# Opening of a hybrid flow step: modulation computed from column blocks on three engines, x of four tiles turned by layout with norms as broadcast rows, loads in a fixed order

## The chip, the cores and the metric

The kernel runs on one core of a Trainium2 chip. A core has a matrix engine (TensorE, PE in the profile), a vector engine (VectorE, DVE), a scalar engine (ScalarE, ACT), a general engine (GpSimd, POOL) and a queue engine (SyncE, SP) that issues most DMAs. Each engine executes its own list of instructions in order and waits on semaphores for the others. The metric is the device time of one execution in microseconds (us). The kernel before took 2190.32 us, the median of three runs (2189.26 to 2190.99).

## The reference

One step of a backbone with two groups of tokens: 128 context tokens (`x_prompt`, conditioned by `c_ctx`) and 2048 latent tokens (`x_sample`, conditioned by `c`). D is 1024. The opening, which is what the change touches, computes for each group

```python
m = jnp.einsum('...d,de->...e', jax.nn.silu(cvec), w) + b      # w is w_ada (1024 x 3072), b is b_ada
shift, scale, gate = jnp.split(m, 3, axis=-1)
xn = rmsnorm(h, ln_g) * (1.0 + scale) + shift                  # h is x; the norm runs over D of each token
proj = jnp.einsum('btd,de->bte', xn, w_in)
```

The columns of `proj` go to three branches: a gated DeltaNet (its q, k, v, decays and the gate `z_a`), a spatial gating MLP, and a Fourier mixer. Each has a SiLU gate path; the branches are projected, merged by sigmoid gates, projected again, and added to x. Outputs are both groups' tokens after a last norm, and the DeltaNet states of the context.

## The kernel before, in words

**Tiles and number format.** The 2176 tokens are cut into five tiles (`TBS`): four of 512 latent tokens (called tiles 0 to 3 here) and one of the 128 context tokens (tile 4). The modulated x lives on chip for the whole kernel, transposed (D on partitions, in 8 blocks k; tokens along the row), as a sum of two 16-bit parts `xh` and `xl`. Weights are split likewise, scaled by a power of two that comes from their sum of squares (`converting`, lines 231 to 252: a ScalarE square with a sum, a small matmul and some one-column VectorE steps in `scales`, a ScalarE scaling that writes the high part, a VectorE pass that writes the low part). A product is three 16-bit matmuls (`gemm_T`, lines 263 to 269): high by high, high by low, low by high.

**The opening, lines 368 to 453.** `c` and `c_ctx` are loaded as 16 rows, transposed by PE, and made to `scT` (SiLU, with D on partitions). The first 2048 columns of `w_ada` come in 8 blocks of 256 columns, each in two loads of 512 KB (line 426) into 8 buffers. PE multiplies `scT` (2 columns, the stationary side) with each 256-wide row block; of blocks 0, 2, 4 and 6 the second half is summed by VectorE (`ada_sum`, lines 407 and 409) and then reduced by PE. The result (2 rows of 256) is copied (line 436) and transposed back in pairs into `pa` (line 438). Ahead of block 4 stand the load of x's first tile and five small loads of parameter columns (`columns`). Lines 443 to 453 then make `sh` and `ms`, the shift and the scale with the norm's gain, bound their size, and scale both by `sx`; `isx` is the reverse factor and goes into every weight's `w.inv` (line 249).

**The silu stage of branch A, lines 456 to 498.** `getw(4)` converts the four weight blocks of `z_a`, and `load_w` those of the decays; both are placed behind the last load of `w_ada` (`issue_after`, which orders instructions of one engine). For each tile: load x with tokens on partitions (line 416), four squares with sums (line 474), a root on GpSimd (line 204), four scalings on VectorE (line 478); for each k, four PE transposes (line 482) into a bank, a VectorE pass that applies `ms` and `sh` (line 484), a ScalarE cast to `xh` (line 485) and a GpSimd subtraction to `xl` (line 486); then for each of four output blocks g a `gemm_T`, a sigmoid (line 491), a product (line 492), and a store to DRAM (line 494).

**What follows.** Lines 631 to 660: 12 output blocks of q, k and v over the five tiles, with the decays worked in between (line 646 is the ScalarE pass that empties a bank). Then the DeltaNet chunks, the other two branches, the merges and the last projection.

**What sets the order.** The program is handed to a scheduler that simulates the engines, takes instructions by priority as their operands come ready, gives out buffers from each pool, and writes a fixed list for each engine. A block under `high_priority` goes ahead. A DMA is placed on the queue of the engine that issues it, and holds that queue while its buffer is taken.

Of the kernel before, what the change touches and what calls it, by code (L numbers as in the profile page):

```python
# [20 lines left out]
P = 128  # L21
# [17 lines left out]
VS = 2048.0  # L39
TBS = [(0, 512), (512, 512), (1024, 512), (1536, 512), (2048, 128)]  # L40
# [88 lines left out]
def _laid_out(inputs):  # L129
# [6 lines left out]
        "w_outb": _by_block(w_out, cols),  # L136
    }

# [6 lines left out]
def hybrid_flow_kernel(ctx: ExitStack, tc: tile.TileContext, x_prompt, x_sample, state_delta, c, c_ctx, ln_g, w_ada,  # L145
                       b_ada, w_blk, w_bd, conv_w, a_log, dt_bias, o_norm_g, sgu_norm_g, w_spatial, b_spatial, w_brb,
                       w_outb, final_g, consts, consts16, y_prompt, y_sample, new_state, dbg=None):
# [37 lines left out]
    SY.dma_start(cst, consts[:, 0:_CF])  # L185
# [39 lines left out]

    def read_w(src, nkt, cols=P, tag="w"):
        st = sb(wp, [P, nkt, cols], "wst" if cols == P else tag + "st", bufs=2 if cols == P else 1)
        SY.dma_start(st, src.rearrange("p (k c) -> p k c", c=cols))
        return st

    def converting(w, st, nkt, cols=P, hi=None, lo=None, tag="w", bufs=5):
# [17 lines left out]
        V.tensor_mul(w.inv, inv, isx)  # L249
        yield  # L250
        A.activation(w.hi, st, AF.Copy, scale=s)  # L251
# [119 lines left out]
    SY.dma_start(prc[0:8, :], c.rearrange("o (k p) -> (o k) p", p=P))  # L371
    SY.dma_start(prc[8:16, :], c_ctx.rearrange("(k p) -> k p", p=P))
    pp = bank(ps_x, [P, 2, KT])
    PE.transpose(pp.rearrange("p g k -> p (g k)"), prc, ident[:16, :16])
    sc = sb(cp, [P, 2, KT], "sc")
    A.activation(sc, pp, AF.Sigmoid)
    scT = sb(cp, [P, KT, 2], "scT")
    V.tensor_mul(scT.rearrange("p k g -> p g k"), sc, pp)
    NPRM = 65
    prm = sb(p0p, [NPRM, P], "prm", bufs=1)  # L380
    pc = sb(cp, [P, NPRM], "pc")

    def columns():
        SY.dma_start(prm[0:8, :], ln_g.rearrange("o (k p) -> (o k) p", p=P))
        SY.dma_start(prm[8:44, :], conv_w[0].rearrange("t (k p) -> (t k) p", p=P))
        SY.dma_start(prm[44:48, :], sgu_norm_g.rearrange("o (k p) -> (o k) p", p=P))
        SY.dma_start(prm[48:49, :], o_norm_g)
        SY.dma_start(prm[49:65, :], b_ada[0, 0:2 * D].rearrange("(k p) -> k p", p=P))
# [30 lines left out]
    for blk in range(8):  # L419
        if blk == XB:  # L420
            load_x(*TBS[0])
            columns()
# [1184 lines left out]
```

## Time and profile before

| | |
|---|---|
| three runs, median | 2190.32 us (2189.26 to 2190.99) |
| the profiled execution | 2187.72 us, span 2185.9 us |
| mean granted clock of PE | 0.991 |
| `w_ada` loads | 16 of 512 KB on SyncE, the first issued at 1.9 us |
| x loads | tile 0 issued at 9.6 us, tile 1 at 30.2, tile 2 at 53.4, tile 3 at 76.2, tile 4 at 105.5 |
| first matmul of the silu stage | 46.58 us |
| first matmul of q, k, v | 152.05 us |

How to read what is quoted further down. The page's part 1 gives the busy time of each engine, its share of the span, and its number of instructions; part 4 the shares of the chain that ended last. A row of stretches has its borders in us, its length, then busy time and number of instructions of PE, PE's weight loads (PEld), DVE, ACT and POOL, then the clock that PE was granted (1.00 is full), the mean busy share of the 16 DMA engines, and GB/s. A row of the timeline has the start, the length, engine, line, operation, what is written and read, shape and count, and in brackets how long the engine stood idle before it and what released it. A row of groups has line, engine, operation, written and read names, shape and count, then total busy time, mean ns of one, and the idle time before. A row of one line's instructions has shortest, median and longest in ns, then the first and last start. A row of waits has the total, the number and the longest in us. A row of DMA issues has the size of one and the us from issue to landing. Line 194 is the helper that issues every matmul.

### The profile page before, as it was taken

The numbers are of one execution on the slowest core, as the hardware profiler recorded it, in microseconds if no ns is written. First come the engines' busy times: TensorE is split into PE (matmuls) and PEld (weight loads), VectorE is DVE, ScalarE is ACT, GpSimd is POOL, SyncE is SP. The second block draws the span as 40 slices with busy tenths as digits, with TensorE's granted clock in tenths as the row PEclk, the third lists the DMA queues.
The fourth block names the chain that finished last, engine by engine and source line by source line (L and its number), as shares of the span: only waits on it lengthen the run. The fifth ranks groups of instructions, "written<-read, shape, count | busy, mean of one in ns | idle before, by whom it ended". The sixth has DMA issues, their size and how long they took to land.

```text
span 2185.9 us, 42789 instructions
## 1 busy us (share of the span) xinstructions
PE 2120.1 (97%) x16327; PEld 1214.5 (56%) x16327; DVE 1320.6 (60%) x3147; ACT 1025.1 (47%) x2365; POOL 721.0 (33%) x893
## 2 busy tenths in 40 slices
PE   7999999999999999999899999999999999999998
PEld 3564444455555577777555555555655444444444
DVE  5736844479878697466655555765674544233454
ACT  3535744365655673455534445655653422222332
POOL 1421332223334332443322223354542222112543
PEclk9999999999999999999899999999999999999999
DMA  8424822167776753444655556766764533334542
GB/s 284 152 87 158 280 100 101 61 212 232 259 214 221 216 166 101 122 131 133 217 158 165 163 157 190 236 188 220 210 198 154 169 122 130 118 102 123 173 149 106
DMA packets 233240, 365.11 MB, mean 167 GB/s; under 512 B 38369, under 2 KB 132938, under 8 KB 230986
## 3 DMA queue, kind: packets, MB, share of 16 engines
q1 hardware_dynamic: 180650, 267.38, 39.2%
q0 software_dynamic: 12688, 51.27, 6.5%
q10 hardware_dynamic: 39696, 43.72, 6.0%
q8 instruction: 128, 2.10, 0.4%
q14 instruction: 78, 0.64, 0.1%
HBM read 234.67 MB, written 127.62 MB: 166 GB/s over the span
## 4 chain that ended last, share of the span: by engine, by line
PE 50%; DVE 6%; DMA 5%; ACT 3%; issue 2%; POOL 1%; ACTq 0%; SPq 0%; POOLq 0%; DVEq 0%
PE b L194 49%; DMA st<-br 1%; DVE XB L814 1%; DVE E L815 1%; DMA wst<-in_w_brb_dram 1%; ACT nd L767 0%; DVE big L1385 0%; ACT big L1384 0%; DVE wlo L252 0%; DMA ei<-XB 0%; DMA wst<-mrg 0%; PE b L1078 0%; DMA wst<-in_w_blk_dram 0%; DMA sn<-n 0%; DMA XB<-nd 0%
## 5 line engine op out<-in xcount | busy, mean ns | idle before, releaser
L194 PE MATMUL b<-xh,whi 128*128 128x512 f16 (+1 forms) x1920 | 653.3, 349 | 6.5 <-DVE sg L1152 4.7
L194 PE MATMUL b<-xl,whi 128*128 128x512 f16 (+1 forms) x1920 | 653.6, 349 | 0.0
L194 PE MATMUL b<-xh,wlo 128*128 128x512 f16 (+1 forms) x1920 | 652.0, 348 | 0.0
L194 PEld LDWEIGHTS <-whi 128*128 128x128 f16 x3904 | 358.0, 98 | 337.7 <-issue 16.5
L194 PEld LDWEIGHTS <-wlo 128*128 128x128 f16 x1952 | 191.9, 98 | 178.5 <-issue 3.6
L194 PE MATMUL b<-big,bhi 128*128 128x512 f16 (+1 forms) x960 | 252.1, 348 | 3.3 <-ACT big L1384 3.1
L1424 POOL TENSOR_TENSOR mrow<-mrow,sg 128x512 f32<-128x512 f32 (+1 forms) x80 | 94.5, 1182 | 287.6 <-DVE sg L1423 171.2
L194 PE MATMUL b<-big,blo 128*128 128x512 f16 (+1 forms) x480 | 163.5, 348 | 0.0
L1414 ACT ACTIVATE sg<-b,winv 128x512 f32<-128x512 f32 (+1 forms) x120 | 74.2, 619 | 165.7 <-PE b L194 165.1
L194 PEld LDWEIGHTS <-xh 128*128 128x128 f16 x1496 | 117.1, 98 | 30.3 <-DVE yT L1337 1.6
L194 PEld LDWEIGHTS <-bhi 128*128 128x128 f16 x960 | 87.3, 98 | 78.6 <-issue 3.5
L655 POOL TENSOR_TENSOR cy<-cy,raw 128x545 f32<-128x545 f32 (+1 forms) x48 | 66.4, 1409 | 186.5 <-ACT raw L654 186.5
L1423 DVE SCALAR_TENSOR_TENSOR sg<-b,binv,sg 128x512 f32<-128x512 f32 (+1 forms) x80 | 53.4, 668 | 103.1 <-PE b L194 93.6
L208 DVE CAST wscb<-wss 128x1 bf16<-128x1 f32 x93 | 14.2, 153 | 157.9 <-ACT wlo L242 66.7
L194 PE MATMUL b<-whi,xh 128*128 128x128 f16 x544 | 92.8, 219 | 2.7 <-DVE yT L1337 1.5
L194 PE MATMUL b<-whi,xl 128*128 128x128 f16 x544 | 92.8, 219 | 0.0
L194 PE MATMUL b<-wlo,xh 128*128 128x128 f16 x544 | 92.8, 219 | 0.0
L194 PE MATMUL b<-wohi,ml 128*128 128x512 f16 (+2 forms) x248 | 91.7, 372 | 0.7 <-DVE ml L1495 0.7
L194 PE MATMUL b<-wohi,mh 128*128 128x512 f16 (+2 forms) x248 | 91.9, 372 | 0.0
L194 PE MATMUL b<-wolo,mh 128*128 128x512 f16 (+2 forms) x248 | 91.9, 372 | 0.0
L887 POOL COPY T<-ES 32x256 f16<-32x256 f16 x68 | 28.8, 423 | 190.3 <-DMA ES<-ei 156.6
L252 DVE SCALAR_TENSOR_TENSOR wlo<-wst,wsc,whi 128x1024 f16<-128x1024 f32 x52 | 72.7, 1401 | 27.9 <-ACT whi L251 27.1
(469 smaller groups left out, 4317.9 us busy)
## 6 DMA issues: line engine op xcount, KB each, us to landing
wst<-in_w_blk_dram SPq DMA_DIRECT2D x60, 512.0 KB, 5.2
qkv<-cy POOLq DMA_DIRECT2D x12, 1089.0 KB, 5.2
st<-br SPq DMA_DIRECT2D x48, 256.0 KB, 4.0
mrow<-mrg SPq DMA_DIRECT2D x18, 512.0 KB, 4.3
mrow<-mrg SPq DMA_DIRECT2D x16, 576.0 KB, 4.3
mrg<-mrow POOLq DMA_DIRECT2D x16, 576.0 KB, 3.7
dc<-dec SPq DMA_DIRECT2D x17, 512.0 KB, 7.0
kq<-qkv SPq DMA_DIRECT2D x34, 256.0 KB, 4.0
```

Of the source, the lines that this page charges most:

```text
L194: PE.matmul(out, l, r, start=start, stop=stop)
L208: V.tensor_copy(sb16, ss)
L252: V.scalar_tensor_tensor(w.lo, st, s, w.hi, ALU.mult, ALU.subtract)
L655: G.tensor_tensor(y[:, c0:c1], y[:, c0:c1], raw[:, 1 + c0:1 + c1], ALU.mult)
L814: V.tensor_tensor(t3, X3[:, 0:k, k:k + 1].to_broadcast([P, k, n_]), E3[:, k:k + 1, k:32].to_broadcast([P, k, n_]), ALU.mult)
L815: V.tensor_tensor(E3[:, 0:k, k:32], E3[:, 0:k, k:32], t3, ALU.subtract)
L887: G.tensor_copy(T16[rows(a0, b), :, :, b], ES[0:32, :, 2 * a0 + b, :, wT])
L1414: A.activation(sg, ps, AF.Sigmoid, scale=gw.inv)
L1423: V.scalar_tensor_tensor(sg, ps, binv[:, 1:2], sg, ALU.mult, ALU.mult)
L1424: G.tensor_tensor(mr, mr, sg, ALU.add)
```

## The change

The host lays out more. `w_ada`'s first 2048 columns come as 16 blocks of 128 columns (`w_adb`), seven of them with D on partitions (for PE), nine transposed, with the output columns on partitions. The parameter columns and both conditioning vectors come as one array of 81 columns (`cols`). x of tiles 1 to 4 comes turned, with D on partitions (`x_t`, `x_tp`); `x_sample` and `x_prompt` are still inputs.

The modulation is computed block by block in the order `ADA_ORDER`: seven blocks on PE (the block is the stationary side, 2 columns move), two on GpSimd (a product with a broadcast row of SiLU, summed by ScalarE), seven on VectorE (product and sum in one instruction). The broadcast rows `rowc` come from 16 small matmuls. x's first tile is loaded behind the third block, scaled by its norms and transposed by PE into `raw0` during the loads. The first two weight blocks of `z_a` are read ahead of the last four blocks and converted without `isx`, which is multiplied into `w.inv` later. Loads pass through `load`, which orders each behind the load before it.

In the silu stage, tile 0 is made from `raw0`. Tiles 1 to 4 are loaded twice, in rows for the norms and turned for the product; the norms become a row that is spread over the partitions (tile 1 by four matmuls, the others through DRAM), and no transposes are made. `silu_za` takes two output blocks at once for tile 0 and for the first pair of tile 1.

```diff
+ADA_PE = (0, 1, 2, 8, 9, 10, 11)
+ADA_G = (3, 12)
+ADA_ORDER = (0, 4, 8, 3, 5, 1, 6, 9, 12, 13, 2, 7, 14, 10, 15, 11)
...
-    SY.dma_start(cst, consts[:, 0:_CF])
+    first = SY.dma_start(cst[:, 0:P], consts[:, 0:P])
...
+    def load(dst, src):
+        if turn_of[0] is None:
+            return SY.dma_start(dst, src)
+        with tc.issue_after(turn_of[0].ins):
+            turn_of[0] = SY.dma_start(dst, src)
+        return turn_of[0]
...
-        V.tensor_mul(w.inv, inv, isx)
+        if isx is None:
+            w.own = inv
+        else:
+            V.tensor_mul(w.inv, inv, isx)
...
+    def norms(xs, shared=False):
+        xss = sb(p0p, [P, len(xs)], "xss")
+        for j, x in enumerate(xs):
+            jk = sb(p0p, [P, D], "xm", F16, bufs=4)
+            if shared and j % 2:
+                V.scalar_tensor_tensor(jk, x, 1.0, x, ALU.mult, ALU.mult, accum_out=xss[:, j:j + 1])
+            else:
+                A.activation(jk, x, AF.Square, accum_out=xss[:, j:j + 1])
+        rs = sb(p0p, [P, len(xs)], "rs")
+        rsqrt(rs, xss, 1.0 / D, len(xs))
+        return rs
...
+    def modulate(b, st):
+        if b in ADA_PE:
+            for k in range(KT):
+                mm(pa[:, ADA_PE.index(b), :], st[:, k * P:(k + 1) * P], scT[:, k, :], k == 0, k == KT - 1)
+            return
+        for g in range(2):
+            if b in ADA_G:
+                prod = sb(p0p, [P, D], "prod", bufs=1)
+                G.tensor_tensor(prod, st, rowc[g], ALU.mult)
+                A.activation(prod, prod, AF.Copy, accum_out=ada[:, b, g:g + 1])
+            else:
+                junk = sb(p0p, [P, D], "xm", F16, bufs=4)
+                V.scalar_tensor_tensor(junk, st, 1.0, rowc[g], ALU.mult, ALU.mult, accum_out=ada[:, b, g:g + 1])
+
+    for i, b in enumerate(ADA_ORDER):
+        if i == 3:
+            x0 = sb(p0p, [P, 4, D], "xt")
+            for j in range(4):
+                load(x0[:, j, :], xrows(j * P, P))
+        if i == 12:
+            read_next()
+            read_next()
+        st = sb(p0p, [P, D], "ab", bufs=8)
+        load(st, w_adb[b])
+        modulate(b, st)
+        if i == 5:
+            rs0 = norms([x0[:, j, :] for j in range(4)])
+            for j in range(4):
+                A.activation(x0[:, j, :], x0[:, j, :], AF.Copy, scale=rs0[:, j:j + 1])
+            for k in range(KT):
+                ps = bank(ps_mm, [P, 512])
+                for j in range(4):
+                    PE.transpose(ps[:, j * P:(j + 1) * P], x0[:, j, k * P:(k + 1) * P], ident)
+                A.copy(raw0[:, k, :], ps)
+    fetch(2)
+    while len(wdone) - len(wsteps) < 2:
+        weight_step()
+    read_next()
+    read_next()
+    x1 = row_blocks(*TBS[1])
...
+    load_xt(1)
+    behind = load(cst[:, P:_CF], consts[:, P:_CF])
+    bdst = read_w(w_bd, KT, 16, "d")
+    turn_of[0] = None
...
+    def row_scale(ti, xs):
+        t0, tn = TBS[ti]
+        rs = norms(xs, ti == 1)
+        if ti == 1:
+            ps = bank(ps_x, [P, 4, P])
+            for j in range(4):
+                mm(ps[:, j, :], rs[:, j:j + 1].to_broadcast([P, P]), ident)
+            rsb = sb(p0p, [P, tn], "rsb", bufs=1)
+            V.tensor_copy(rsb, ps.rearrange("p j t -> p (j t)"))
+            return rsb
+        G.dma_start(rsD[t0:t0 + tn].rearrange("(j p) -> p j", p=P), rs)
+        rsb = sb(p0p, [P, tn], "rsb", bufs=1)
+        SY.dma_start(rsb, rsD[None, t0:t0 + tn].to_broadcast([P, tn]))
+        return rsb
+
+    for ti, (t0, tn) in enumerate(TBS):
+        g = 0 if t0 < NS else 1
+        for k in range(KT):
+            hi, lo = xh[:, k, t0:t0 + tn], xl[:, k, t0:t0 + tn]
+            if ti:
+                x = xts[ti][:, k, :]
+                V.scalar_tensor_tensor(x, x, ms[:, k, g:g + 1], rsb, ALU.mult, ALU.mult)
+                act = A.activation(hi, x, AF.Identity, bias=sh[:, k, g:g + 1])
+                if k == 2:
+                    made = act
+                if k % 2:
+                    G.tensor_scalar(x, x, sh[:, k, g:g + 1], None, ALU.add)
+                    G.tensor_tensor(lo, x, hi, ALU.subtract)
+                else:
+                    with tc.high_priority() if ti == 1 else ExitStack():
+                        V.scalar_tensor_tensor(lo, x, sh[:, k, g:g + 1], hi, ALU.add, ALU.subtract)
+                continue
+            made = A.activation(hi, raw0[:, k, :], AF.Identity, scale=ms[:, k, g:g + 1], bias=sh[:, k, g:g + 1])
+            t = sb(p0p, [P, 512], "xm", bufs=4)
+            of = V.tensor_scalar(t, raw0[:, k, :], ms[:, k, g:g + 1], sh[:, k, g:g + 1], ALU.mult, ALU.add)
+            (V if k % 2 else G).tensor_tensor(lo, t, hi, ALU.subtract)
+        if ti == 0:
+            zaw.extend(wdone[:2])
...
+            silu_za(0, (0, 1), others)
...
+            with tc.issue_after(zaw[3].made.ins):
+                rsb = row_scale(1, x1)
+                bdw = convert(bdst, KT, 16, hi=bdp[:, :, 0:16], lo=bdp[:, :, 16:32], tag="d")
+            silu_za(0, (2, 3))
+        else:
+            if ti < 4:
+                xs = row_blocks(*TBS[ti + 1])
+                load_xt(ti + 1)
+            for gs in ((0, 1),) if ti == 1 else ((0,), (1,)):
+                silu_za(ti, gs)
+            if ti < 4:
+                with tc.issue_after(made.ins):
+                    rsb = row_scale(ti + 1, xs)
+            for g in range(2, 4):
+                silu_za(ti, (g,))
...
-    SY.dma_start(wsn, w_spatial[0].rearrange("g p q -> p g q"))
+    with tc.issue_after(behind.ins):
+        SY.dma_start(wsn, w_spatial[0].rearrange("g p q -> p g q"))
```

`others`, called inside the first `silu_za` at its sixth k, converts the third and fourth weight block of `z_a`, placed behind the last passes that make tile 0. `row_blocks` loads the rows of a tile as blocks of 128 tokens, `load_xt` the turned x of a tile.

171 lines of the change are left out of this document (81 added, 90 removed).

## The prediction

> **What bounds the kernel now.** I read the page first. The engine line says that PE is busy 97% of the span and that no other engine comes near; the chain that ended last is half PE matmul on line 194. So a stage is worth what it costs PE, in matmuls issued or in gaps.
>
> ```profile
> span 2185.9 us, 42789 instructions
> PE 2120.1 (97%) x16327; PEld 1214.5 (56%) x16327; DVE 1320.6 (60%) x3147; ACT 1025.1 (47%) x2365; POOL 721.0 (33%) x893
> PE 50%; DVE 6%; DMA 5%; ACT 3%; issue 2%; POOL 1%; ACTq 0%; SPq 0%; POOLq 0%; DVEq 0%
> ```
>
> Then I cut the opening into stretches (busy time per engine, granted clock, DMA share, GB/s).
>
> ```profile
> 0.00:10.00 10.00, 3.57 (x9) 1.19 (x10) 2.09 (x7) 1.47 (x2) 0.61 (x9) 1.00 0.81 258
> 10.00:20.00 10.00, 10.00 (x45) 3.86 (x44) 4.80 (x13) 0.00 (x0) 0.00 (x0) 1.00 1.07 375
> 20.00:35.00 15.00, 11.35 (x55) 4.31 (x53) 9.75 (x25) 4.60 (x8) 1.18 (x1) 1.00 1.08 350
> 35.00:40.00 5.00, 5.00 (x26) 2.04 (x24) 0.85 (x4) 2.30 (x4) 0.00 (x0) 1.00 1.02 406
> 46.00:48.00 2.00, 2.00 (x10) 1.56 (x11) 2.00 (x3) 2.00 (x5) 1.40 (x1) 0.55 0.00 0
> 0.00:153.00 153.00, 138.03 (x764) 71.17 (x765) 90.71 (x198) 70.69 (x127) 50.36 (x60) 0.99 0.52 181
> 153.00:435.00 282.00, 282.00 (x1776) 141.25 (x1775) 160.27 (x190) 140.26 (x203) 75.28 (x90) 1.00 0.40 139
> ```
>
> Up to 40 us the DMA engines are full: loads set the pace. From 153 us PE is full for 282 us, so work that reaches line 646 earlier keeps its lead there. In between lies the silu stage of branch A. Its corners are in the timeline:
>
> ```profile
> 34.76 1.89 PE L194 MATMUL b<-ast,scT 128*2 128x256 f32 x8 [1.41 <-DMA ast<-in_w_ada_dram]
> 41.59 0.17 DVE L443 TENSOR_TENSOR sh<-b,pc 128x16 f32<-128x16 f32 x1 [0.84 <-PE b L438]
> 43.91 0.23 DVE L453 TENSOR_SCALAR sh<-sh,xsc 128x16 f32<-128x16 f32 x1
> 46.58 0.59 PE L194 MATMUL b<-xh,zhi 128*128 128x512 f16 x1
> 152.05 0.38 PE L194 MATMUL b<-xh,whi 128*128 128x512 f16 x1
> ```
>
> The modulation is ready at 43.91 + 0.23 = 44.1 us, although PE's last wait for a piece of w_ada ended at 34.8: about 9 us go into matmuls, VectorE sums, copies and transposes behind the loads. The silu stage then runs to 152.05, which is 107.9 us. What PE must issue in it:
>
> ```profile
> L194 PE MATMUL b<-xl,zhi 128*128 128x512 f16 x128 | 48.2, 382 | 0.7 <-POOL xl L486 0.7
> L194 PE MATMUL b<-xl,zhi 128*128 128x128 f16 x32 | 5.3, 219 | 0.0
> 44.00:152.00 108.00, 18.27 (x124) 14.91 (x124) 0.98 0.35 122
> 90.22 0.38 PE L194 MATMUL b<-xh,zhi 128*128 128x512 f16 x1
> 91.30 0.38 PE L194 MATMUL b<-xh,zlo 128*128 128x512 f16 x1
> 96.92 1.25 PE L482 MATMUL b<-cst,xt 128*128 128x128 f32 x10
> ```
>
> Five steps lie between 90.22 and 91.30, 0.216 us each. Three products of 128 make 384 x 0.216 = 82.9 us; the 96 narrow ones are a quarter as wide, 5.3 us by width. The third row is line 482 alone: 124 transposes in the stage. Ten run in 1.25 us of which the last one's own 0.27 us is latency, so 0.109 us each and 13.5 us in all. Together 101.7 us; the other 6.2 us are gaps, mostly between 44 and 60 us, where tile 0 is made while PE waits and the clock stands at 0.55.
>
> **The change part by part.**
>
> *Modulation ready.* Ahead of the last column block now stand 0.12 MB of small loads, 16 blocks of 0.524 MB, x's first tile with 2.10 MB and two weight blocks with 1.05 MB: 11.65 MB. The first 10 us moved 2.58 MB; the remaining 9.07 MB take 22.3 us at 406 GB/s, 25.9 at 350, so the block lands between 32.3 and 35.9. I take 375 GB/s: 34.2. Behind it come eight f32 matmuls with a 128-column stationary side. The nearest row loads such weights:
>
> ```profile
> 174.32 0.85 PEld L194 LDWEIGHTS b<-tok,cst 128*128 128x128 f32 x6
> L1577 DVE SCALAR_TENSOR_TENSOR hh<-hh,hss,fg 128x1024 f32<-128x1024 f32 x16 | 21.5, 1349 | 13.4 <-POOL hss L204 13.3
> L1517 POOL TENSOR_TENSOR gt<-gb,inv 128x1024 f32<-128x1024 f32 x16 | 31.3, 1956 | 9.6 <-DMA gb<-gate 9.6
> L474 ACT ACTIVATE jk<-xt 128x1024 f16<-128x1024 f32 x17 | 17.9, 1051 | 19.3 <-DMA xt<-in_x_sample_dram 18.4 <-DMA xt<-in_x_prompt_dram 0.8
> L485 ACT CAST xh<-xm 128x512 f16<-128x512 f32 x32 | 19.2, 613 | 17.4 <-DVE xm L484 17.0
> ```
>
> 0.85 / 6 = 0.14 us each, 1.1 us for eight, and 7.9 us for all 56 among the loads. The VectorE block lands one block (1.4 us) before the last and takes two passes of 1.35 us, so it ends 1.3 us behind the last landing. From there the small chain that took 44.1 - 41.6 = 2.5 us stays: 34.2 + 1.3 + 2.5 = 38.0. The other VectorE passes (seven blocks, 14 x 1.35 = 18.9 us) replace sums of like size and stand under 30 us of loading; GpSimd's four products (4 x 1.96 = 7.8 us) too. ScalarE is the tight one, in order: four copies of broadcast rows, four squares, four scalings, eight copies of transposed x, four sums of products, two weight squares and two scalings, that is 16 of 1.05 and 12 of 0.61, 24 us and some read-outs between 6 and 38 us. Any late operand delays the rest. I put 1 us on it and take 39.0, a gain of 5.1. Bounds: all loads at the fast rate, 36.1 (gain 8.0); ScalarE behind until 44 (gain 0).
>
> The rate hangs on the layout: the slow stretch (350) held w_ada in pieces of 1 KB a row, the fast one (406) weights and x in 4 KB. [...]
>
> *Transposes leave PE.* The stage loses 124 x 0.109 = 13.5 us and gains four 128-column f32 matmuls that spread the norm of tile 1 (4 x 0.14 = 0.6). Net 12.9. Twenty of the 124 belong to tile 0 and partly filled gaps; if they were free, 104 x 0.109 - 0.6 = 10.7 is left.
>
> *Gaps of the stage.* The rows for one pass of each engine:
>
> ```profile
> L486 POOL TENSOR_TENSOR xl<-xm,xh x40: 426/1157/2262, 46.6 to 149.3; 128x512 f16<-128x512 f32 x32, 128x128 f16<-128x128 f32 x8
> L491 ACT ACTIVATE sg<-b,winv 128x512 f32<-128x512 f32 x16 | 10.7, 682 | 19.5 <-PE b L194 19.5
> L492 DVE SCALAR_TENSOR_TENSOR sg<-b,winv,sg 128x512 f32<-128x512 f32 x16 | 11.7, 744 | 13.9 <-ACT sg L491 13.9
> ```
>
> Tile 0 comes now from x already turned: per k one ScalarE pass (0.61), one VectorE pass, and a subtraction on GpSimd or VectorE. PE starts about 0.7 us behind the modulation, waits about 1.3 us for the first low part (a GpSimd pass), runs some 3 us at half clock as it did (loss 1.5), waits once for a bank when the second pair begins (ScalarE 0.7 and VectorE 0.7), and about 1 us for the third and fourth weights, whose loads wait on the first two's buffers. On SyncE the rows and the turned x of tile 1 stand behind that wait: issued near 37, the 5.2 MB take 14 us and are there by 51, while PE wants them at 39 + 24 = 63. That is 5.9 against 6.2 before: gain 0.3. Bounds: all of that hidden but the start (gain 4), or twice it (loss 6).
>
> *Tiles 1 to 4 made from turned x.* Per wide tile: VectorE 8 products and 4 low parts at about 0.75, ScalarE 8 passes of 0.61 and 4 squares of 1.05 with read-outs, GpSimd 4 additions and 4 subtractions of 1.16. VectorE 9, ScalarE 10, GpSimd 9 us, under the 96 x 0.216 = 20.7 us that PE needs for the tile. That cover makes them free; it is gone only where a tile's making starts late, as in two rivals below. SyncE reads each stored norm back and holds the silu stores and the qkv weights behind that wait, which nobody needs before the stage ends. Loads double (rows for the norm, turned x for the product): 4.2 MB a tile, 11 us at 375 GB/s, under 20.7 too; the stage's DMA share was 0.35.
>
> The rest (constants in two parts, columns laid out by the host, the held spatial weights) lies under loads and is worth 0 within 1 us.
>
> Sum: 5.1 + 12.9 + 0.3 = 18.3 us. The profiled execution took 2187.72 us, 1.8 around its span; it would take 2169.4. The median of the three runs shown is 2.6 above it, so I forecast 2190.3 - 18.3 = 2172.0. All bounds together: gain from 0 + 10.7 - 6 = 4.7 to 8 + 12.9 + 4 = 24.9.
>
> **Rivals.**
>
> *The opening is held by ScalarE, not by loads* (chance 0.13). Then only the transposes are won: 2190.3 - 13 = 2177. For it: 24 us in strict order. Against: by the stretches above it was busy 1.5 of the first 20 us, so its work can spread out.
>
> *VectorE and GpSimd exclude each other* (0.12). In the row of line 486 above the same subtraction takes from 1.16 us (the median) to 2.26. If each GpSimd pass must wait out VectorE's and the reverse, a tile costs 9 + 9 = 18 us in sequence, 2.3 us per k against the 1.3 in which PE eats one when it takes two output blocks at once in tile 1: some 6 us of waits there, and tile 0 likewise about 3. Time 2190.3 - 18.3 + 9 = 2181. [...]
>
> *Loads of the next tile come late* (0.10, the slower side). They stand on SyncE's queue among stores of the silu results, which wait for VectorE:
>
> ```profile
> SPq L494 <- DVE sg L492: 56.6, 16, 13.1
> 53.39 0.38 SPq L416 DMA_DIRECT2D xt<-in_x_sample_dram  x1
> 76.17 0.38 SPq L416 DMA_DIRECT2D xt<-in_x_sample_dram  x1
> nd<-nd POOLq DMA_DIRECT2D x34, 64.0 KB, 2.9
> dc<-gamR SPq DMA_DIRECT2D x16, 256.0 KB, 4.0
> ```
>
> From issue to a usable tile: rows land 5.6 us later (2.1 MB), last square 1.2, root on GpSimd about 1.2, the norm stored (at least 2.9, like nd) and read back spread (4.0, like dc), product, high and low part 2.1: 17 us. A tile lasts 20.7, so 3.7 us are spare. If the loads are issued 15 us into the tile before, tiles 2, 3 and 4 wait 11 us each: 34 - 18.3 = 16 us slower, 2206. It decides from about 10 us late per tile. Against it: before, the loads went out a tile and more ahead (53 and 76 us for tiles 2 and 3), and there are now buffers for two tiles of rows and two of turned x.
>
> *The order behind the opening shifts* (0.05). The scheduler places every queue's instructions anew, and PE's gaps behind 153 us are (2185.9 - 153) - (2120.1 - 138.0) = 51 us; if a third grows back, the result is 2190. No row speaks for it, and a few us either way belong to the range.
>
> **How the numbers follow.** My forecast holds 0.60. Its own range is 2165 to 2180, from the bounds with the extremes dropped. The two rivals that keep a part reach 2181, and a shift of some us behind it 2186; late loads and a lost gain lie beyond. I leave those 0.15 out and a little at the fast end: 2163 to 2186. This measurement tells about 0.2% (4.4 us) from no change. Faster: 0.60 + 0.13 + 0.12 less a little = 0.84; same 0.05; slower 0.11.
>
> **What would show it.** The pass that scales sh ends near 39 us rather than 44.1; the first qkv matmul starts near 134 us rather than 152; no transpose of x after the modulation; wide matmuls 0.216 us apart through tiles 1 to 4, with no PE wait over 2 us at a tile's start; the stage from 153 on as long as before. [...] The forecast is wrong if the opening is shorter as said and the end is not.

## The result, and the profile after

The changed kernel is slower: 2227.01 us median of four runs (2222.15 to 2231.78) beside 2190.65 us of the kernel before (2189.26 to 2195.79), ratio 1.0162, interval 1.0134 to 1.0189. The profiled execution took 2222.15 us. The span and the busy times from its page, and the shares of the chain:

```profile
span 2220.2 us, 42676 instructions
PE 2120.9 (96%) x16245; PEld 1226.4 (55%) x16245; DVE 1330.2 (60%) x3145; ACT 1042.1 (47%) x2386; POOL 737.6 (33%) x896
PE 47%; DVE 7%; DMA 5%; ACT 3%; issue 2%; POOL 1%; ACTq 0%; SPq 0%; POOLq 0%; DVEq 0%
```

PE issues 82 matmul instructions fewer and is busy just as long (2120.9 for 2120.1 us), and 34.3 us of span are added around that. Where they sit is read from stretches with the two corners of the text: the modulation ready, and the first matmul of the DeltaNet chunks behind q, k and v (from here on "the corner"). First the kernel before, then the changed one; columns as in the prediction.

```profile
0.00:44.10 44.10, 32.07 (x145) 12.81 (x145) 20.05 (x66) 9.23 (x19) 1.79 (x10) 1.00 0.96 327
44.10:449.00 404.90, 401.96 (x2459) 205.98 (x2460) 236.80 (x341) 208.63 (x326) 128.25 (x145) 1.00 0.39 136
```

```profile
0.00:49.40 49.40, 38.51 (x179) 37.65 (x180) 28.88 (x58) 26.34 (x45) 11.98 (x14) 1.00 0.74 271
49.40:486.40 437.00, 400.51 (x2343) 195.19 (x2343) 239.64 (x347) 208.18 (x320) 132.41 (x144) 0.96 0.41 145
```

The opening is 5.3 us longer. Between the corners it is 32.1 us longer: PE's gaps went from 2.9 to 36.5 us, and its busy time fell by only 1.5 us though 12.9 us of transposes (net, at the prediction's price) are gone. Behind the corner the changed kernel is 3.1 us shorter.

**The opening.** The timeline of PE in the changed kernel, and then three groups and two rows of single lines:

```profile
12.41 13.81 PE L222 MATMUL b<-scT,ab 128*128 128x2 f32 x64
37.71 3.41 PE L222 MATMUL b<-scT,ab 128*128 128x2 f32 x16
40.98 2.80 PE L509 MATMUL b<-cst,xt 128*128 128x128 f32 x12
43.58 3.41 PE L222 MATMUL b<-scT,ab 128*128 128x2 f32 x16
50.73 0.63 PE L222 MATMUL b<-xh,zlo 128*128 128x512 f16 x1
51.16 0.63 PE L222 MATMUL b<-xh,zhi 128*128 128x512 f16 x1
```

```profile
L222 PE MATMUL b<-scT,ab 128*128 128x2 f32 x112 | 24.1, 350 | 0.0
L509 PE MATMUL b<-cst,xt 128*128 128x128 f32 x32 | 7.8, 426 | 1.1 <-ACT xt L505 1.1
L222 PE MATMUL b<-prc,cst 16*128 16x128 f32 x32 | 7.2, 421 | 5.3 <-DVE prc L422 5.3
L222 PEld LDWEIGHTS b<-scT,ab x112: 288/333/338, 12.4 to 46.6; 128*128 128x128 f32 x112
L544 DVE TENSOR_SCALAR sh<-sh,xsc x1: 228/228/228, 49.2 to 49.2; 128x16 f32<-128x16 f32 x1
```

A column block is 16 instructions, not 8 (56 matmuls are x112), and takes 3.41 us. Tile 0's transposes and the broadcast blocks (the 16 small matmuls that make `rowc`, 32 instructions) add 15 us of PE. From 36 us to the last block PE goes from block to transposes to block without a pause. The first wide matmuls step by 0.43 us where the stage's step is 0.216: PE is at half clock there, although the clock column of the stretch says 1.00.

**The silu stage.** Waits; the steps of one tile's norm with what it holds up, in the timeline; a stretch, and the landing of the stores:

```profile
DVE xt L594 <- DMA rsb<-rs: 26.1, 3, 10.9
PE b L222 <- DVE sg L567: 12.0, 3, 8.4
PE b L222 <- ACT whi L293: 9.3, 1, 9.3
PE b L222 <- DVE wscb L236: 6.0, 1, 6.0
```

```profile
114.01 0.85 POOL L583 DMA_DIRECT2D rs<-rs  x1
122.52 0.33 SPq L585 DMA_DIRECT2D rsb<-rs  x1
128.48 2.74 DVE L594 SCALAR_TENSOR_TENSOR xt<-xt,ms,rsb 128x512 f32<-128x512 f32 x4 [10.86 <-DMA rsb<-rs]
139.28 0.59 PE L222 MATMUL b<-xh,zhi 128*128 128x512 f16 x1 [8.40 <-DVE sg L567]
```

```profile
130.00:140.00 10.00, 1.60 (x7) 0.55 (x5) 10.00 (x13) 7.13 (x12) 9.25 (x5) 0.68 0.18 64
DMA to landing us min/median/max: 8.1/8.5/10.9
```

The store of the norms takes 8.5 us to land, the read back 6 us more (4.5 in the tile before). The earlier tile's norm was usable at 101.36, this one at 128.48: 27.1 us for a tile that PE works off in 20.7. In between lie, one behind the other, the third high part (done at 104.2), four squares (to 108.3, with no wait for a row of x), the root on VectorE and GpSimd, in turn with low parts, the store (issued at 114.0, landed at 122.5) and the read back. VectorE stands at the first product and the products that empty PE's banks (line 567) stand behind it, so PE waits "for sg" and restarts at half clock (steps of 0.43 us until 143.5). The wait of 6.0 us for `wscb`, a weight's scale, is the same stand one tile earlier: VectorE comes to it at 110.5, behind the eight products that began at 101.36.

### The profile page after: what moved, and what is told of

The parts are those of the page before. It is cut to its first block, busy times and chain, and to the rows that moved or that the text cites. A ratio compares the mean times of both kernels' runs of the same rounds, so it can differ in the third digit from the quotient of the medians.

```text
span 2220.2 us, 42676 instructions
## 1 busy us (share of the span) xinstructions
PE 2120.9 (96%) x16245; PEld 1226.4 (55%) x16245; DVE 1330.2 (60%) x3145; ACT 1042.1 (47%) x2386; POOL 737.6 (33%) x896
## 4 chain that ended last, share of the span: by engine, by line
PE 47%; DVE 7%; DMA 5%; ACT 3%; issue 2%; POOL 1%; ACTq 0%; SPq 0%; POOLq 0%; DVEq 0%
PE b L222 46%; DMA st<-br 1%; DVE XB L952 1%; DVE E L953 1%; DMA ei<-XB 1%; DMA wst<-in_w_blk_dram 1%; DMA wst<-in_w_brb_dram 0%; DMA xr<-in_x_sample_dram 0%; DVE big L1523 0%; ACT nd L905 0%; DVE wlo L294 0%; DMA XB<-nd 0%; DVE sv L1140 0%; DMA of<-sz 0%; PE b L1216 0%
## 5 line engine op out<-in xcount | busy, mean ns | idle before, releaser
L1552 ACT ACTIVATE sg<-b,winv 128x512 f32<-128x512 f32 (+1 forms) x120 | 74.3, 619 | 164.3 <-PE b L222 163.9
```

The costliest lines, as they stand in the source:

```text
L1552: A.activation(sg, ps, AF.Sigmoid, scale=gw.inv)
```

## The experiments

A delta in us is the difference of two ratios to before, times 2188 us. The corner is from each profiled execution, which is one run of several: e4's was its slowest, h2's its fastest.

| kernel | ready | corner | ratio to before |
|---|---|---|---|
| before | 44.1 | 449.1 | 1 |
| after | 49.4 | 486.6 | 1.0162 (1.0134 to 1.0189) |
| e1 norms by matmuls | 49.0 | 469.5 | 1.0093 (1.0077 to 1.0110) |
| e2 tiles 1 to 4 as before | 49.0 | 450.1 | 1.0016 (1.0006 to 1.0025) |
| e3 store from SyncE | 48.2 | 485.0 | 1.0156 (1.0141 to 1.0171) |
| e4 norms a tile earlier | 49.0 | 475.8 | 1.0109 (1.0093 to 1.0124) |
| f1 = e1 + weights ahead | 48.3 | 460.0 | 1.0088 (1.0073 to 1.0103) |
| f2 = e1 + squares behind | 49.4 | 478.6 | 1.0136 (1.0116 to 1.0155) |
| f3 = e1 + low parts on VectorE | 48.4 | 465.9 | 1.0064 (1.0049 to 1.0079) |
| f4 = e1 + old modulation | 45.7 | 462.8 | 1.0065 (1.0050 to 1.0080) |
| g2 = f3 + f4 | 45.5 | 457.2 | 1.0055 (1.0040 to 1.0071) |
| g1 = f1 + f3 + f4 | 45.5 | 441.7 | 0.9996 (0.9985 to 1.0007) |
| g3 = g1 + norms a tile earlier | 46.6 | 445.8 | 1.0002 (0.9992 to 1.0012) |
| h1 = g1, rows once | 45.6 | 444.5 | 0.9999 (0.9986 to 1.0012) |
| h2 = after, rows once | 48.7 | 470.8 | 1.0139 (1.0121 to 1.0157) |
| h3 = g1, tile 1 as before | 45.8 | 444.9 | 0.9981 (0.9971 to 0.9991) |
| g4 = e2 + old modulation | 45.8 | 447.8 | 0.9984 (0.9974 to 0.9994) |
| k3 = f1 + f3 | 47.7 | 451.5 | 0.9999 (0.9987 to 1.0010) |
| k1 = k3 + 12 matmuls ahead | 48.2 | 447.0 | 1.0000 (0.9987 to 1.0013) |
| k2 = k1 + 36 between | 48.5 | 448.9 | 1.0003 (0.9990 to 1.0016) |

From the corner to the end PE's work is the same, yet the kernels differ by some us either way (before 1736.8 us, f1 1742.6, g1 1741.0, g4 1732.5, and all others between g4's and 1742.9 of h1); nothing here explains that. So a gain at the corner is not yet a gain in time.

### The spread norm (e1, e3, e4, h2)

e1 spreads every tile's norm as tile 1's:

```diff
-        if ti == 1:
-            ps = bank(ps_x, [P, 4, P])
+        nt = tn // P
+        ps = bank(ps_x, [P, nt, P])
...
-        G.dma_start(rsD[t0:t0 + tn].rearrange("(j p) -> p j", p=P), rs)
...
-        SY.dma_start(rsb, rsD[None, t0:t0 + tn].to_broadcast([P, tn]))
```

> The changed kernel with one thing else: the norms of tiles 2, 3 and 4 are spread over the partitions by matmuls against the identity, as those of tile 1 already are, and no longer go through device memory. Theory A (the spread norm's way through device memory, with VectorE's products waiting for it in order ahead of the products that empty PE's banks, takes 27.1 us per tile where PE has work for 20.7): the stage loses its gaps, the first qkv matmul comes near 460 instead of 486, the time is 2195 to 2203. Theory B (x is loaded twice, and the loads or their collisions set the pace): the waits move to the loads of x, the time stays at 2214 to 2224. Theory C (VectorE and GpSimd hold each other up at their port, so the making itself is too slow): the period per tile stays above 24 us, 2210 to 2222.

15 us less than the changed kernel, and the waits for the spread norm are gone. It is less than theory A expected: the corner fell by 17 us and stays 20 us behind the kernel before.

e3 changes one engine: `SY.dma_start(rsD...)` for `G.dma_start(rsD...)`.

> The changed kernel with the store of the norms issued by SyncE instead of GpSimd. Theory A1 (what makes the store late is GpSimd's queue: its descriptors and the low parts ahead of it): the store is issued 2 to 4 us earlier and lands sooner, the gap per tile shrinks from 6 to 11 us to 3 to 6, 2208 to 2216. Theory A2 (the 4-byte pieces themselves take 8 to 11 us to land and the chain behind one tile's making is what counts): landing stays at 8 us or more, 2218 to 2230.

No change (1.3 us, inside the interval). The norm's store and its read back:

```profile
L583 SPq DMA_DIRECT2D rs<-rs x3: 319/371/377, 82.6 to 140.0; - x3
L585 SPq DMA_DIRECT2D rsb<-rs x3: 319/323/327, 91.2 to 147.5; - x3
```

The first store goes out at 82.6 instead of 85.9, but the read back can follow only 8.6 us later, in the next tile 12.7 and in the last 7.5. GpSimd's queue was not the cause; A2.

e4 keeps the way through DRAM and makes it early:

```diff
+    x2 = row_blocks(*TBS[2])
...
-                rsb = row_scale(1, x1)
+                rsbs = {1: row_scale(1, x1)}
+                rsbs[2] = row_scale(2, x2)
...
-                xs = row_blocks(*TBS[ti + 1])
+                if ti < 3:
+                    xs = row_blocks(*TBS[ti + 2])
```

> The changed kernel with the way through device memory kept, but the rows of a tile loaded and their norms made one tile earlier (two buffers for the spread norm; one scratch buffer less). Theory A: the latency of store and read back is the same 8 to 11 us and 2 us, but a whole tile of 20.7 us covers it; VectorE no longer waits for the spread norm, the time is 2196 to 2206, like the matmul variant. Theory B (loads of x twice): no gain or a loss, 2214 to 2228. Theory C (the port): period per tile above 24 us, 2210 to 2222.

The store lands slower still, and it matters less (landing, and PE's longest wait):

```profile
DMA to landing us min/median/max: 9.4/11.7/12.0
PE b L222 <- ACT whi L293: 16.5, 3, 12.6
```

11.6 us are won though the latency rose, 5 to 15 us less than expected; the wait for a q, k, v weight's high part, 9.3 us in the changed kernel, is 16.5 here.

h2 drops the second load of tiles 2 to 4: `xs = x1[0:TBS[ti + 1][1] // P]`.

> The changed kernel as it is, the spread norms still through device memory, but without the second load of tiles 2 to 4 in the same way (their right norms are left out). Theory A: the store and the read back still stand behind one tile's making, ratio to before 1.015 to 1.018, within 3 us of the changed kernel. Theory B: the store lands sooner because no loads stand in its way, 1.009 to 1.013.

5.0 us are won, just outside both expectations. The landing is the same (median 8.8 us), so the loads were not what made the norms late; the wait for the q, k, v weight's high part is what is missing in this profile. The second load has a part in the loss, by another way; at the corner of the profiled execution it is 15.8 us, but 9 of them come back behind it.

### The opening and the new tiles apart (e2, f4, g4)

e2 keeps the new opening and tile 0, and makes tiles 1 to 4 as before:

```diff
-                x = xts[ti][:, k, :]
-                V.scalar_tensor_tensor(x, x, ms[:, k, g:g + 1], rsb, ALU.mult, ALU.mult)
+                ps = bank(ps_d, [P, tn])
+                for j in range(tn // P):
+                    PE.transpose(ps[:, j * P:(j + 1) * P], xts[ti][:, j, k * P:(k + 1) * P], ident)
```

> The new opening with tile 0 as in the changed kernel, but tiles 1 to 4 made as before: rows loaded once, scaled by VectorE, transposed on PE. Theory of the opening (PE's float32 column blocks at 3.4 us each make the modulation 5.3 us later, tile 0's 32 transposes that move in front of it are worth 3.5 us behind it): the time is 2190.5 + 5.3 - 3.5 = 2192, 2189 to 2197, and the modulation is ready at 49 to 50. If the new tiles are not what costs (rival: the new order of the weights' conversion and the loads in fixed order delay the stage whatever the tiles are), 2205 or more.

As expected: 3.5 us over the kernel before (interval 1.3 to 5.5). So of 35 us, 32 come with the tiles from the layout when the new opening stands in front of them.

f4 takes e1 and puts the old loop over `w_ada` back (two columns stationary, 256 moving, half blocks on VectorE), with tile 0's scalings and transposes ahead of the last block.

> The variant with norms spread by matmuls, and the modulation made as before (two columns stationary, 256 columns of the weights moving, four half blocks on VectorE), with x of tile 0 still transposed ahead of it. Theory of the opening (PE's float32 column blocks and the spread rows hold the opening back): the modulation is ready at 42 to 46 instead of 49.4, ratio to before 1.005 to 1.008, 4 to 8 us less than the matmul variant. Rival (tile 0's transposes and copies ahead of the modulation cost what the blocks cost): ready at 48 or later, ratio 1.009 or more.

Ready at 45.7 instead of 49.0, and 6 us less in the end. That is more than the 3.3 us of the opening; where the rest comes from is not shown. g4 joins f4's opening with e2's tiles.

> Old modulation and tiles 1 to 4 as before (scaled by VectorE, transposed on PE), only tile 0 scaled and transposed ahead of the modulation, with the loads in fixed order. The modulation is ready 1 to 2 us later than in the kernel before, tile 0's 32 transposes behind it (3.5 us) go: ratio to before 0.998 to 1.000. If the fixed order of loads or the shifted weights cost something by themselves: 1.001 to 1.003.

0.16% (3.5 us) faster than the kernel before, as expected, and 7 us less than e2, which differs in the opening alone. What g4 keeps of the change (tile 0 scaled and transposed during the loads, the fixed order, two weights converted early) pays by itself.

### VectorE and GpSimd (f3)

```diff
-                if k % 2:
-                    G.tensor_scalar(x, x, sh[:, k, g:g + 1], None, ALU.add)
-                    G.tensor_tensor(lo, x, hi, ALU.subtract)
-                else:
+                if True:
```

> The variant with norms spread by matmuls; the low parts of the odd blocks of tiles 1 to 4 are made by VectorE in one instruction each (0.70 us) instead of by GpSimd in two. Theory C (VectorE and GpSimd hold each other at their port): VectorE's eight products take 5.4 us instead of 9.9 us where GpSimd used to run, the making of a tile shortens although VectorE has 2.8 us more to do, ratio to before 1.004 to 1.008. If the port is not what counts: VectorE's added 2.8 us per tile show or nothing does, ratio 1.009 to 1.013.

6.3 us less than e1. The product of a tile, in e1 and then in f3 (groups, 44 to 160 us):

```profile
L590 DVE SCALAR_TENSOR_TENSOR xt<-xt,ms,rsb 128x512 f32<-128x512 f32 (+1 forms) x32 | 28.1, 944 | 0.1
L595 POOL TENSOR_SCALAR xt<-xt,sh 128x512 f32<-128x512 f32 (+1 forms) x16 | 25.0, 1567 | 28.5 <-ACT xh L591 28.5
```

```profile
L596 DVE SCALAR_TENSOR_TENSOR xl<-xt,sh,xh 128x512 f16<-128x512 f32 (+1 forms) x32 | 19.1, 649 | 0.4 <-ACT xh L591 0.4
L590 DVE SCALAR_TENSOR_TENSOR xt<-xt,ms,rsb 128x512 f32<-128x512 f32 (+1 forms) x32 | 18.7, 649 | 0.0
```

These means mix 24 wide and 8 narrow passes; the 24 of 128x512 take 1.132 us on average in e1 and 0.750 in f3. The same 32 products take 18.7 instead of 28.1 us once GpSimd makes no low parts beside them: the 16 low parts that VectorE takes over (8.2 us more) cost less than the 9.4 us it lost to GpSimd, and the norms' root no longer queues behind low parts (PE's wait for it: 3.2 us in e1, 0.6 in f3). How the 6.3 us divide between the two was not separated. The rows show that the products take longer beside GpSimd's low parts; that a port is the reason was my assumption, and no run shows it.

### The place of the squares (f2)

In e1 ScalarE runs the next tile's four squares between the third and the fourth high part. f2 moves the earliest place: `if k == 7:` for `if k == 2:` where `made` is set.

> The variant with norms spread by matmuls; the next tile's norms may be issued only behind the tile's eighth high part instead of its third. In the matmul variant ScalarE runs four squares (4.9 us) between the third and the fourth high part, and PE waits 3.1 us for a low part at 81 and 3.2 us for the norms' root at 103. Theory E (the place of the squares in ScalarE's order makes the high parts late): the first wait goes, 3 to 6 us less than the matmul variant, ratio to before 1.0065 to 1.008. Rival: the norms are now too late for the next tile, VectorE's products start late, the time is the same or up to 10 us more, ratio 1.009 to 1.014.

9.4 us more than e1, the rival: PE's waits moved to low parts (4.9 us) and to sg (3.0), and the wait for a q, k, v weight grew from 9.9 to 16.5 us.

### The weights of q, k and v (f1, g1, g2)

In 220 to 240 us VectorE is full or nearly full in all kernels (16.5 to 20.0 of 20 us). Stretches of the kernel before and of e1:

```profile
220.00:240.00 20.00, 20.00 (x113) 9.84 (x112) 19.87 (x15) 14.85 (x19) 10.31 (x8) 1.00 0.77 255
```

```profile
220.00:240.00 20.00, 12.39 (x77) 6.28 (x74) 20.00 (x14) 13.06 (x16) 10.83 (x10) 0.91 0.80 263
PE b L222 <- ACT whi L293: 9.9, 1, 9.9
```

Decays, convolution and the scaling of the next weight share VectorE there. In the kernel before a weight's scaling ends there at 241.7 and PE does not wait; in e1 one ends at 242.3, and PE, which is further on, has waited 9.9 us for it. f1 converts three weights between the silu groups:

```diff
+            ahead(3)
...
                 silu_za(ti, (g,))
+                weight_step()
```

> The variant with norms spread by matmuls, and the first three qkv weight blocks converted in steps between the silu groups of tiles 1 to 4 instead of at the stage's end. In the matmul variant PE waits 9.9 us for a qkv weight's high part near 232, and again some us at half clock, because VectorE is full from 200 to 250 with the decays, the convolution and the conversion; the kernel before reaches that point about 10 us later and never waits. Theory D (PE, relieved of transposes, runs into a stretch that VectorE bounds, and weights converted earlier carry it over): the wait goes and the time falls by 8 to 13 us against the matmul variant, ratio to before 1.003 to 1.006. If VectorE's stretch simply cannot be passed (the next conversion is late in turn): within 4 us of the matmul variant, ratio 1.007 to 1.011.

The wait is gone and the corner is 9.5 us earlier, as theory D has it, but the ratio fell by only 1.1 us, inside the intervals: in the profiled executions 5.5 us came back behind the corner. By the ratio alone it would have counted against D. g2 joins f3 and f4, and g1 all three.

> The same without the weights converted ahead. If opening and port add: 1.0093 - 0.0028 - 0.0029 = 1.0036, 1.002 to 1.005. If an earlier silu stage only makes the wait for the qkv weight near 220 longer (theory D): 1.005 to 1.008, with that wait above 14 us.

> Norms spread by matmuls, the old modulation, all low parts of tiles 1 to 4 on VectorE and the first three qkv weights converted between the silu groups, together. If the three losses stand beside each other (opening 6 us, port 6 us, qkv weight 1 to 9 us against the matmul variant at 1.0093): ratio to before 0.999 to 1.003. If the gains run into the stretch that VectorE bounds near 220 to 240 and vanish there: 1.004 to 1.007. Below 0.998 it would beat the kernel before.

g2 wins only 8.3 of the 12.4 us that f3 and f4 win singly; its wait for the weight is 10.1 us (not over 14 as expected) and its PE in 220 to 240 is at 9.54 of 20 us. g1 is 12.9 us better than g2 by the same edit that gave 1.1 us in f1:

```profile
220.00:240.00 20.00, 9.54 (x30) 3.68 (x31) 20.00 (x22) 14.65 (x18) 8.38 (x8) 0.66 0.80 273
```

```profile
220.00:240.00 20.00, 20.00 (x107) 9.48 (x106) 19.97 (x19) 16.91 (x21) 10.81 (x8) 1.00 0.81 291
45.50:441.60 396.10, 390.50 (x2361) 194.58 (x2361) 242.79 (x367) 207.50 (x320) 95.50 (x109) 1.00 0.45 162
```

First g2, then g1, whose last row runs from its modulation to its corner. PE is busy 390.5 us there, 11.5 less than before, with gaps of 5.6: what leaves PE does arrive once nothing else holds it, 8.8 us up to the corner. Behind it 4 us are lost again, and the total is even with the kernel before.

### What is left in g1 (g3, h1, h3)

g3 adds e4's earlier norms to g1.

> As the three together, and the norms made a whole tile earlier with the rows (two buffers for the spread norm, one scratch buffer less). If what is left in the silu stage is the place of the squares: 2 to 6 us less than the three together. If the loads of two tiles' rows behind the opening delay the weights instead: equal or up to 6 us more.

No gain, so neither the place of the squares nor a late norm is what is left. h1 drops the second load of rows from g1 by the line of h2.

> The three together, but the rows of tiles 2, 3 and 4 are not loaded: the norms of these tiles are made again from tile 1's rows, with the same squares and matmuls. This leaves the right norms of tiles 2 to 4 out. Theory B (x loaded twice keeps the transfers at full share from 48 to 80 and makes weights and tile 1's parts late): PE's waits of 2.3 us and 2.3 us in the silu stage shrink, ratio to before 0.997 to 0.9985. If the second load is hidden: 0.999 to 1.0005, the same as the three together.

Equal within the intervals: the second load is hidden in g1. h3 makes tile 1 as before inside g1.

> The three together, but tile 1 made as before: its rows loaded once, scaled by VectorE and transposed on PE (3.5 us of PE), tiles 2 to 4 from the layout. If what tile 1 waits for is the double load in the opening's wake, its 2.3 us waits go and PE's 3.5 us come: 0.9985 to 1.0000, about even with the three together. If the wake's loads cost more than these waits (weights, clock after idle): below 0.998, faster than both kernels. If PE's transposes simply come on top: 1.0005 to 1.002.

0.9981, the fastest beside g4, between the first two expectations: 3 us under g1, with overlapping intervals. Tile 1's transposes cost nothing there that shows.

### PE's clock in the opening (k1, k2, k3)

k3 is the control, g1 with the new modulation.

> The control of these two: new modulation, norms spread by matmuls, low parts on VectorE, first qkv weights converted between the silu groups, no added matmuls. Against the three together with the old modulation (0.9996) the opening alone differs: if it costs what it cost in the matmul variant, ratio 0.9996 + 0.0028 = 1.0024, 1.001 to 1.004, modulation ready at 48 to 49.5.

0.9999, below what was expected: with the rest mended the new opening costs nothing that can be measured in the total, though its modulation is 2.2 us later and its corner, in the profiled execution, 9.8 us later than g1's.

```diff
+    def busy(n):
+        for _ in range(n):
+            PE.matmul(wps, ones16, ones16[:, 0:1].to_broadcast([P, 512]), start=True, stop=True)
+    busy(12)
```

> New modulation, norms spread by matmuls, low parts on VectorE, first qkv weights converted between the silu groups, and ahead of everything twelve 16-bit matmuls of 512 columns (added work, its result unused), while PE waits for the first load. In the changed kernel PE runs the whole opening and on to 55 us at half clock: float32 weight loads take 333 and 230 ns where others take 141, wide steps 0.43 us. Theory W1 (only the start is cold, and once at full speed the column blocks keep it): weight loads in the opening at 141 to 200 ns, modulation ready at 42 to 46, ratio 2 to 4 us below the same kernel without the twelve. Theory W2 (matmuls that move two columns do not count as work enough to hold the clock): it falls back within some us, ready at 48 to 50, ratio the same.

```profile
1.00 4.32 PE L224 MATMUL b<-ones 128*128 128x512 bf16 x12 [1.00 <-POOL ones L217]
5.25 5.09 PE L229 MATMUL b<-prc,cst 16*128 16x128 f32 x32
...
0.00:10.00 10.00, 9.00 (x44) 6.24 (x44) 1.60 (x4) 3.46 (x6) 0.61 (x9) 0.88 0.71 261
10.00:20.00 10.00, 9.08 (x43) 8.77 (x42) 4.36 (x5) 4.71 (x8) 3.04 (x2) 0.50 1.01 407
L229 PEld LDWEIGHTS b<-scT,ab x112: 288/333/338, 10.3 to 45.4; 128*128 128x128 f32 x112
L229 PEld LDWEIGHTS b<-prc,cst x32: 181/185/328, 5.2 to 9.7; 16*128 16x128 f32 x32
```

W2 by its outcome. The broadcast blocks start at 185 ns a weight load. The granted clock was 0.88 over the first 10 us and 0.50 over the next; if it fell once, it fell at about 7.6 us (an estimate from the 0.88), while they still ran. The column blocks behind them run at 333 ns, though PE is busy 9.08 of the next 10 us. So k1 shows that the broadcast blocks did not hold the clock and that the column blocks did not raise it; whether column blocks hold a clock that they find is seen only in k2. The changed kernel's 333 ns are thus half clock from its first matmul on, which the clock column shows as 1.00. k2 puts the same matmul between.

> As the one with twelve matmuls ahead, and besides one such matmul behind every second float32 matmul of the column blocks and two behind each broadcast block (36 more, 0.216 us each at full clock, 7.8 us of PE). Theory W2: these hold the clock, a weight load takes 141 ns, a block 2.3 us + 4 x 0.216 = 3.1 us instead of 3.4, the transposes 0.14 instead of 0.23; ready at 45 to 48, and tile 0 starts at full clock (0.216 us steps from its first), together 3 to 5 us less than without. If the clock does not rise (the price is the float32 weight load itself in this place): a block 3.4 + 1.7 us, ready above 52, 5 us more or worse.

```profile
17.26 3.65 PE L229 MATMUL b<-scT,ab 128*128 128x2 f32 x32
20.76 2.72 PE L224 MATMUL b<-ones 128*128 128x512 bf16 x6
23.28 4.05 PE L229 MATMUL b<-scT,ab 128*128 128x2 f32 x32
43.83 2.23 PE L229 MATMUL b<-scT,ab 128*128 128x2 f32 x16
30.00:40.00 10.00, 8.44 (x42) 8.11 (x42) 9.67 (x21) 9.36 (x17) 3.17 (x2) 0.50 0.76 304
```

At full clock a block takes 1.8 us (two in 3.65) instead of 3.41. Behind these two blocks the six added matmuls took 0.42 us each ((23.28 - 20.76) / 6), where 0.216 is full speed: the clock had fallen by about 20.8 us, so the blocks do not hold it either. The scheduler placed all added matmuls before 23.3 us, and from 30 to 40 the clock was 0.50. It rose once more under the last block, which took 2.23 us instead of 3.41, behind twelve transposes at half clock; in the changed kernel and in k1 the block behind the same twelve took 3.41, and why is open.

All column blocks together took 16.8 us of PE in k2 instead of 24.1, and still the modulation came no earlier. Ahead of its last blocks PE waits for a weight's scale from VectorE, to 35.8 us in k2 and to 35.5 in the changed kernel, and VectorE is busy 9.67 of the 10 us from 30 to 40 in both; the stretch behind that wait ran at half clock again. What an opening at full clock to its end would give stays open.

## Why the prediction was wrong

**Modulation ready, gain 5.1.** Measured: a loss of 5.3. The step that failed is "0.85 / 6 = 0.14 us each, 1.1 us for eight, and 7.9 us for all 56". The row's six loads were three matmuls of two instructions each, and the price was one at full clock. Measured 3.41 us for eight and 24.1 for all. Two terms stood at nothing on PE: the broadcast blocks (7.2 us) and tile 0's transposes, which the change moves into the opening (7.8). The loads, which were to set the pace, moved 387 GB/s from 10 to 20 us (375 before), but fell to a DMA share of 0.74 over the opening, since their buffers were held (SyncE waited 11.4 us for PE's column blocks). PE, with 38.5 us of work in 49.4, took the place that I gave to ScalarE (26.3): from 36 to 47 us it works on end at half clock, and VectorE waits 3.5 us for it. VectorE, full from 30 to 40, had its part in what came before. In this run the column blocks alone ran 13.8 us on end at half clock, 0.213 us an instruction: these float32 matmuls with two moving columns did not raise the clock.

**Transposes leave PE, gain 12.9.** They left, and between the corners PE's busy time fell by 1.5 us only; the rest went into half clock behind the new gaps (mean granted clock 0.96 instead of 1.00). In g1, without those gaps, PE's busy time falls by 11.5 us, and 8.8 arrive at the corner; g1's ratio of 0.9996 shows none of them at the end, and that part stays open. Up to the corner mechanism and size were right, the condition (PE kept fed) was not.

**Tiles made free under 20.7 us.** This step ("That cover makes them free") failed, and it decided the case. The sum of 9, 10 and 9 us a tile says nothing on order: the chain from squares through store, read back, product and high part is serial, begins only inside the tile before, and VectorE waits for it in front of work that PE needs. It made a tile 27.1 us. e1 and e4 take it away in two different ways and win 15 and 11.6 us.

**The rival of late loads (2206, 0.10)** had this chain nearly whole, with the same consequence, and was given too little: I took the store at 2.9 us from the row of a 64 KB store, measured 8.5 for one of 2 KB in pieces of 4 bytes. Its reason, loads held on SyncE, was not the cause: the squares waited for no row, and in h2, without those loads, VectorE waited for the spread norm as long as before (27.4 us beside 26.1).

**The rival of VectorE and GpSimd (2181, 0.12)** was at work beside the others: 6.3 us (f3), of which the root's queue has a part. The median of 1.16 us in its row counts eight narrow passes; the 32 wide ones took 1.32 us on average in the kernel before. In e1 a wide product took 1.13 us, where the sum had 0.75, and a wide addition on GpSimd 1.87, where it had 1.16. That each pass waits out the other engine's in full, as its sum assumes, no run shows.

**Gaps 0.3, and "the stage from 153 on as long as before".** Wrong: PE waited 9.3 us for a q, k, v weight's high part. "PE is full for 282 us, so work that reaches line 646 earlier keeps its lead" was read from PE alone; VectorE was just as full from 200 to 240, and PE had come late enough not to meet it. This is worth 1 us when other losses stand in front (f1) and 13 when they don't (g1 beside g2).

Two readings of the profile looked like a rival. VectorE's product waited 26.1 us for the spread norm, and PE for what stood behind it, as under late loads. The modulation at 49.4 us lay beyond the bound of 44 for a late ScalarE, but the engine that was late was PE. The forecast's range ended at 2186, since all bounds were taken on terms of the sum, and the only way to a loss stood outside it.

## What to carry to other kernels

Work that replaces PE's must be checked as a chain, from the first operand to the bank, not as a sum of busy time; the place where an in-order engine waits for the slow link is what PE pays (here 8.4 us, to 139.28). Here a value of a few bytes per partition was spread faster by matmuls than through DRAM: in the changed kernel tile 1's norm was usable 4.7 us after its root (69.6 to 74.3), those of tiles 2 and 3 through DRAM 17.0 and 16.2 us after theirs (84.4 to 101.4, 112.3 to 128.5). With a whole tile's time for it, the way through DRAM won 11.6 us (e4), the matmuls 15 (e1), with overlapping intervals. Before a gain is carried into the next stage, look at which second engine is full there: here the lead was kept only as far as that engine's work could be moved ahead, and the repairs showed their worth only together.

## What the runs showed of the hardware

- Float32 matmuls with a 128-column stationary side and two moving columns: two instructions each, 0.213 us an instruction at half clock, 0.114 at full (3.65 / 32). 13.8 us of them on end did not raise the clock (changed kernel), and in k2, after 3.65 us of them at full clock, the wide matmuls behind them took 0.42 us each instead of 0.216.
- The clock column showed 1.00 through the changed kernel's opening, and 0.50 for the same work in k1, where the clock had risen and fallen before; the step between like matmuls (0.43 or 0.216 us) tells it.
- Stores of 128 x 4 float32 in 4-byte pieces landed 8.5 to 12.0 us after their issue on GpSimd's queue, those of 128 x 1 7.7 to 9.4 (changed kernel, e4, h2); on SyncE's the read back was issued 8.6 and 12.7 us after the 128 x 4 stores and 7.5 after the 128 x 1 (e3).
- A 128x512 float32 product with two operands in SBUF took VectorE 0.750 us on average without GpSimd's low parts (f3) and 1.132 beside them (e1); with the narrow ones the means are 0.649 and 0.944.
